# Output projection of a decoder trunk: x loaded behind the next operands, four sums of squares together, turns a step later, U2 added to the rows by GpSimd

## The chip, the cores and the metric

The kernel runs on one core of one Trainium2 chip. The metric is the device time of one execution in microseconds; the lower the better. A core has TensorE (matmuls and transposes, into eight banks of PSUM), VectorE, ScalarE, GpSimd and SyncE (SP), which here only issues DMAs. Each engine runs its own instructions in order and waits on semaphores of the others.

## The reference

One layer of a hybrid decoder trunk on 1024 tokens of width 1024, in float32. What matters here is the end of the token-mixing sub-layer and the norm behind it:

```python
def rmsnorm(x, g):
    xf = x.astype(jnp.float32)
    y = xf * lax.rsqrt(jnp.mean(xf * xf, axis=-1, keepdims=True) + RMS_EPS)
    return (y * g.astype(jnp.float32)).astype(x.dtype)
...
    x = x + merged @ w_o
    h2 = rmsnorm(x, norm2_g)
    g_ff, up_ff = jnp.split(h2 @ w_gate_up, 2, axis=-1)
    return x + (jax.nn.silu(g_ff) * up_ff) @ w_down
```

`merged` (the four mixers' branches, weighed by gates) is 1024 x 1024, and so is `w_o`.

## The kernel before, in words

Each float32 matmul is made of three: both operands are split into a high part (a cast on ScalarE, L143) and a low part (the difference, on VectorE, L144), and hi·hi, lo·hi and hi·lo are added up in PSUM (L138 to L140). `split` and `split2` do this for operands in `hi`/`lo` tiles or in halves of `ohl`.

The output projection `outproj` multiplies 2 x 2 blocks of 512 with seven block products instead of eight (Winograd's form). The list `OUT` has 28 steps: each is one product (na, nb) and one of four slices j of its inner dimension. A step has four tiles t of 128 rows and three matmuls for each, so 12 matmuls. I number the steps from 0. Steps 0 to 7 are the products 0 and 1, mixed, and then come the products 4 (steps 8 to 11), 3 (12 to 15), 6 (16 to 19), 5 (20 to 23) and 2 (24 to 27). A product has four banks of PSUM, `acc`, and after its last step each of the four is read out and added to what it belongs to.

The sums go into two sets of rows that were loaded from x: `x2[0]`, the first 512 tokens as four tiles of 128 x 1024, and `x2[1]`, the second 512. In the profile these tiles are called raw. A partial sum `u` is kept in the tile `part`: product 0, then U2 (product 4 added), later product 5. `x0` and `x1` are a row tile's two halves of columns.

`want_o(fetched, ready)` issues the operands' loads on SP (L997 the left half from `mfd` in DRAM, L998 the right half from `wo` or `wod`) up to eight steps ahead, and their splits up to six steps ahead. x is loaded by `load_x2`, four DMAs of 512 KB on SP (L850); the norm's weights `g2`, spread over 128 partitions, by one DMA on ScalarE's queue (L1042).

When a row tile of the first half is complete (after product 6), `norm2_first` normalizes and turns it: a square with its sum on ScalarE (L168), the power −1/2 on GpSimd (L164, behind a small VectorE instruction, L163), the scaling on VectorE (L1060, output xn), eight 128 x 128 transposes on TensorE (L1054, output trn), two copies out of PSUM (L1071) and their split into g0h and g0l. A copy f of the turned rows is kept. `beside(n)`, called in step 20 + n, advances these four generators: one tile a step is normalized, and is turned in the step after. In the steps 25 to 27 it prepares the first weights of the feed-forward layer. Behind `outproj` come twelve products on the first half's rows alone (`early`), beside which the second half is normalized and turned, and then the feed-forward layer's main loops.

What sets the order: loads stand on SP in the order of the code. Of the other engines' instructions a scheduler makes the final order when the program is built, by the order of the code, by dependencies and by a buffer pool: tiles of tag b share 14 buffers, and a tile waits for the last reader of the buffer that it takes. In `early` alone the matmuls and transposes are held in the order of the code.

Of the kernel before, what the change touches and what calls it, by code (L numbers as in the profile page):

```python
# [37 lines left out]
ALU = mybir.AluOpType  # L38
AX = mybir.AxisListType

P = 128
# [11 lines left out]
def tile_hybrid_trunk(  # L53
# [17 lines left out]
    nc = tc.nc  # L71
# [14 lines left out]
    def big(name, tag="b", dt=F32):  # L86
        return mn.tile([P, 1024], dt, tag=tag, name=name, bufs=NB[tag])
# [4 lines left out]
    def halves(v):  # L92
        return [v[:, :512], v[:, 512:]]
# [41 lines left out]
    def mm3(o, a, b, start, stop):  # L135
        ah, al = a
        bh, bl = b
        nc.tensor.matmul(o, ah, bh, start=start, stop=False)  # L138
        nc.tensor.matmul(o, ah, bl, start=False, stop=False)  # L139
        nc.tensor.matmul(o, al, bh, start=False, stop=stop)  # L140

    def split(hi, lo, v):
        nc.scalar.copy(hi, v)  # L143
        nc.vector.tensor_sub(lo, v, hi.bitcast(F32))  # L144
# [17 lines left out]
    def rstd_of(ss, n):  # L162
        nc.vector.tensor_scalar(ss, ss, 1.0 / n, EPS, op0=ALU.mult, op1=ALU.add)  # L163
        nc.gpsimd.tensor_tensor(ss, ss, nhalf[:, :ss.shape[1]], op=ALU.pow)  # L164

    def norm_stat(xt, xn):
        ss = sp.tile([P, 1], F32, name="ss")
        nc.scalar.activation(xn, xt, AF.Square, accum_out=ss)  # L168
        rstd_of(ss, D)
        return ss  # L170
# [9 lines left out]
    def h_tiles(name):  # L180
        hh = hp.tile([P, NK, HT], F32R, tag="hh", name=name + "h")
        hl = hp.tile([P, NK, HT], F32R, tag="hl", name=name + "l")
        return hh, hl
# [623 lines left out]
    add, sub, mul, tt = ALU.add, ALU.subtract, ALU.mult, nc.vector.tensor_tensor  # L807
    def bank(name):
        return pq.tile([P, HT], F32, tag="bank", name=name, bufs=8)
# [38 lines left out]
    def load_big(src):  # L848
        raw = big("raw")
        nc.sync.dma_start(raw, src)  # L850
        return raw

    def blocks_w(row0, row1, first=True):

        r0, r1 = load_big(row0), load_big(row1)
        s23, s14 = big("s23"), big("s14")
        s = halves(s14)[:1] + halves(s23) + halves(s14)[1:]
        four(s, *halves(r0), *halves(r1), True)
        w = {}
        if first:  # L860
            x = split2(r0)
            w[1], w[2] = half_of(x, 0), half_of(x, 1)
        x = split2(s23)
        w[6], w[7] = half_of(x, 0), half_of(x, 1)
        x = split2(s14, "b")
        w[5], w[3] = half_of(x, 0), half_of(x, 1)
        w[4] = halves(big("a22", "b", F32R))
        split(*w[4], halves(r1)[1])
        return w
# [123 lines left out]
    def want_o(fetched, ready):  # L993
        for na, nb, j in OUT[len(oraw):fetched]:
            r = big("or")
            if j < 3 or na > 1:
                nc.sync.dma_start(r[:, lo_], mfd[j][:, na])  # L997
            nc.sync.dma_start(r[:, hi_], wo[(0, 0, 1)[nb], j][:, (lo_, hi_, hi_)[nb]] if nb < 3 else wod[j][:, nb])  # L998
            oraw.append(r)
        for i in range(len(oops), min(ready, len(OUT))):  # L1000
            if i % 8 < 2:
                oops.append(split2(oraw[i]))
            else:
                v = t8([2, 1024], "ohl")
                oops.append([v[:, 0], v[:, 1]])
                split(*oops[i], oraw[i])

    load_x2 = lambda half: [load_big(x[half * HT + t * P:half * HT + (t + 1) * P, :]) for t in range(4)]
# [29 lines left out]
    stash = [dp.tile([P, D], F32, name=f"stash{g}") for g in range(EARLY)]  # L1038
    ffd = [dp.tile([P, 7, HT], F32, name=f"ffd{j}") for j in range(NF // 2)]
    wdd = [dp.tile([P, 7, HT], F32, name=f"wdd{j}") for j in range(NF // 2)]  # L1040
    g2 = big("g2")
    nc.scalar.dma_start(g2, norm2_g.partition_broadcast(P))  # L1042
    x2 = [load_x2(0), None]
    hA = h_tiles("g0")
    part = hp.tile([P, 8, HT], F32, tag="hl", name="part")
    hB = h_tiles("g1")
# [3 lines left out]
    def turn(xn, b):  # L1050
        tr = bank("trn")
        for k in range(4):
            kk = 4 * b + k
            nc.tensor.transpose(c4(tr)[:, k, :], xn[:, kk * P:(kk + 1) * P], identf)  # L1054
        return tr

    def norm2(x2):
        xn = big("xn2")
        ss = norm_stat(x2, xn)
        nc.vector.scalar_tensor_tensor(xn, x2, ss, g2, op0=ALU.mult, op1=ALU.mult)  # L1060
        return xn

    def norm2_first(t, x2):

        c = slice(t * P, (t + 1) * P)
        xn = norm2(x2)
        yield
        f1.append(big("f1"))
        for b in range(2):
            f = halves(f1[t])[b]  # L1070
            nc.scalar.copy(f, turn(xn, b))  # L1071
            split(hA[0][:, 4 * b:4 * b + 4, c], hA[1][:, 4 * b:4 * b + 4, c], c4(f))
            yield

    def norm2_second(t, x2):

        c = slice(t * P, (t + 1) * P)
        xn = norm2(x2)
        yield
        f11, f21 = halves(f1[t])  # L1080
        s = halves(big("s12")) + halves(big("s34"))
        tt(s[0], turn(xn, 0), f11, op=sub)
        split(hB[0][:, 0:4, c], hB[1][:, 0:4, c], c4(s[0]))
        yield
        tr = turn(xn, 1)
        tt(s[1], tr, s[0], op=sub)
        split(hB[0][:, 4:8, c], hB[1][:, 4:8, c], c4(tr))
        tt(s[2], s[1], f11, op=sub)
        tt(s[3], f21, s[1], op=sub)
        for v, to in zip(s[1:], (F.t2, F.t3, F.t4)):  # L1090
            split(to[0][:, :, c], to[1][:, :, c], c4(v))
        yield

    def outproj(after):
        u, u4 = ([part[:, i + t] for t in range(4)] for i in (0, 4))
        accs = {}
        for i, (na, nb, j) in enumerate(OUT):
            want_o(i + 8, i + 6)
            if na not in accs:
                accs[na] = [bank("acc") for _ in range(4)]  # L1100
            X = accs[na]
            for t in range(4):
                tl = slice(t * P, (t + 1) * P)
                mm3(X[t], [v[:, tl] for v in oops[i]], [v[:, hi_] for v in oops[i]], j == 0, j == 3)
            for t in range(4) if j == 3 else ():
                x0, x1 = (v and halves(v[t]) for v in x2)
                if na == 0:
                    nc.scalar.copy(u[t], X[t])
                    nc.gpsimd.tensor_tensor(x0[0], x0[0], u[t], op=add)
                elif na == 1:  # L1110
                    tt(x0[0], X[t], x0[0], op=add)
                elif na == 4:
                    tt(u[t], X[t], u[t], op=add)
                elif na == 3:
                    tt(u4[t], X[t], u[t], op=add)
                    tt(x1[1], X[t], x1[1], op=add)
                    nc.gpsimd.tensor_tensor(x0[1], x0[1], u4[t], op=add)
                elif na == 6:
                    tt(x0[1], X[t], x0[1], op=add)
                    nc.gpsimd.dma_start(x2d[t], x2[0][t])  # L1120
                elif na == 5:
                    tt(u[t], X[t], u[t], op=add)
                else:
                    tt(x1[0], X[t], x1[0], op=add)
                    for c in x1:
                        tt(c, c, u[t], op=add)
                    nc.gpsimd.dma_start(x2d[4 + t], x2[1][t])
            if i == 8:
                x2[1] = load_x2(1)
            if i >= 20:  # L1130
                after(i - 20)

    def prepared(f):
        return split2(load_big(wgu[f]))
# [10 lines left out]
        nc.gpsimd.dma_start(stash[g], st)  # L1145

    up_w = lambda g: blocks_w(wgu[2 * g], wgu[2 * g + 1], g >= EARLY)
    turns = [norm2_first(t, x2[0][t]) for t in range(4)]
    ready = []

    def beside(n):

        if n < 4:
            next(turns[n])
        if 0 < n < 5:
            next(turns[n - 1])
            next(turns[n - 1])
        if n >= 5:
            ready.append(prepared(2 * (n - 5)))

# [4 lines left out]
    turns = [norm2_second(t, x2[1][t]) for t in range(4)]  # L1165
# [77 lines left out]
    v, u = (hp.tile([P, 8, HT], F32, tag="hl", name=n) for n in ("pu", "ug"))  # L1243
# [68 lines left out]
    def pool_add(o, v):  # L1312
        nc.gpsimd.tensor_tensor(o, o, v, op=add)
# [8 lines left out]
    with in_order([(nc.tensor, "matmul"), (nc.scalar, "copy"), (nc.scalar, "activation"), (nc.sync, "dma_start")]):  # L1322
        X = product(0, each(load_xr))
        for t in range(4):
            nc.scalar.copy(p1[t], X[t])
        X = product(1, each(load_xr, range(4, 8)) + each(lambda t: pool_add(xr[t][:, lo_], p1[t])))
        for t in range(4):
            tt(xr[t][:, lo_], X[t], xr[t][:, lo_], op=add)
        X = product(2, each(lambda t: first_half(t, lo_)))
        for t in range(4):  # L1330
            tt(u2[t], X[t], p1[t], op=add)
        X = product(3)
# [4 lines left out]
        X = product(4)  # L1337
# [4 lines left out]
        X = product(5, each(lambda t: first_half(4 + t, hi_)))  # L1342
        for t in range(4):
            tt(xr[4 + t][:, lo_], X[t], xr[4 + t][:, lo_], op=add)
        X = product(6, each(last_half), stagger=6)
    with in_order():
# [5 lines left out]
        x, ss = xr[3], ssf[3]  # L1352
# [74 lines left out]
```

## Time and profile before

| what | value |
|---|---|
| median of 3 runs | 1564.3 us (1563.82 to 1564.4) |
| the profiled execution: time, span of its instructions | 1562.95 us, 1561.2 us |
| granted TensorE clock | 0.998 |
| busy share of the span: TensorE, VectorE, ScalarE, GpSimd | 99%, 78%, 43%, 13% |
| output projection, first matmul to the first behind it | 834.2 to 921.0 us |

The times in the trace are microseconds from the start of the span. A row of the timeline has the start, the length, the engine, the line of the kernel, the operation, output and inputs by their names, and in brackets how long the engine was idle before it, and what ended that. A matmul's length is longer than the distance to the next one's start, since matmuls are pipelined; what it takes of the engine is that distance. A count at the end (x4) tells how many equal instructions were merged into one row.

### The profile page before, as it was taken

The page shows a single profiled execution, that of the slowest core. Times are in us where ns is not written, and L with a number is a line of the kernel's source. Part 1 is how long each engine was busy: PE and PEld are TensorE (multiplying, and loading weights), DVE is VectorE, ACT ScalarE, POOL GpSimd, SP SyncE. Part 2 cuts the span into 40 slices and gives each one's busy share as a digit, 9 for nine tenths or more (in the row PEclk, how much of TensorE's full clock was granted, in tenths as well). Part 3 has the DMA queues.
Part 4 walks back from the last instruction along what each step waited for, and adds up shares of the span by engine and source line. Part 5 has one row for each costly group of instructions (what it writes and reads, how often), then busy time and mean ns, then how long its engine had stood idle before and what let it go on. Part 6 is the DMA issues. An engine that isn't in the chain of part 4 may idle for free.

```text
span 1561.2 us, 20401 instructions
## 1 busy us (share of the span) xinstructions
PE 1540.8 (99%) x7362; PEld 1274.3 (82%) x7362; DVE 1212.7 (78%) x1811; ACT 663.6 (43%) x1083; POOL 203.3 (13%) x327
## 2 busy tenths in 40 slices
PE   9999999999999999999999989999999999999998
PEld 8878878888788888888887878888888888888887
DVE  7585687786966878888986878888898888666566
ACT  6343355664666633333333456321222222354343
POOL 2011021221122100000001221000011111110410
PEclk9999999999999999999999999999999999999999
DMA  5221311101346744545447755355465555998612
GB/s 190 71 78 35 103 34 37 34 23 34 128 153 221 270 133 150 184 148 182 155 162 260 269 206 189 141 196 183 162 222 209 209 211 214 342 409 310 191 55 108
DMA packets 94456, 258.05 MB, mean 165 GB/s; under 512 B 11185, under 2 KB 16465, under 8 KB 94354
## 3 DMA queue, kind: packets, MB, share of 16 engines
q1 hardware_dynamic: 73104, 182.80, 34.8%
q0 software_dynamic: 20816, 72.63, 11.7%
q8 instruction: 58, 0.95, 0.2%
q10 hardware_dynamic: 434, 1.32, 0.2%
q14 instruction: 44, 0.36, 0.1%
HBM read 177.25 MB, written 79.45 MB: 164 GB/s over the span
## 4 chain that ended last, share of the span: by engine, by line
PE 86%; DVE 5%; issue 4%; DMA 2%; ACT 2%; POOL 0%; SPq 0%; DVEq 0%; ACTq 0%; POOLq 0%
PE acc L154 13%; PE pp L138 13%; PE pp L140 13%; PE pp L139 13%; PE mm L138 5%; PE mm L140 4%; PE mm L139 4%; PE pp L154 4%; PE o L512 2%; PE trp L499 2%; PE mmz L154 1%; PE pc L139 1%; PE pc L140 1%; PE z L441 1%; PE acc L139 1%
## 5 line engine op out<-in xcount | busy, mean ns | idle before, releaser
L143 ACT CAST hi<-s 128x1024 fp32r<-128x1024 f32 x76 | 76.7, 1050 | 182.1 <-DVE s L823 166.5
L154 PE MATMUL acc<-dhl 128*128 128x512 f32 (+1 forms) x558 | 125.8, 382 | 0.0
L154 PEld LDWEIGHTS acc<-dhl 128*128 128x128 f32 x558 | 102.5, 188 | 20.4
L144 DVE TENSOR_TENSOR lo<-s,hi 128x1024 fp32r<-128x1024 f32 x76 | 90.1, 1221 | 13.5 <-ACT hi L143 13.4
L144 DVE TENSOR_TENSOR dhl<-dr,dhl 128x1024 fp32r<-128x1024 f32 x45 | 58.5, 1312 | 34.0 <-ACT dhl L154 34.0
L890 ACT ACTIVATE g<-g 128x512 f32<-128x512 f32 x38 | 23.9, 629 | 125.9 <-DVE g L889 113.4
L144 DVE TENSOR_TENSOR lo<-raw,hi 128x1024 fp32r<-128x1024 f32 x46 | 55.9, 1219 | 22.5 <-ACT hi L143 22.5
L138 PE MATMUL mm<-h0h,whi 128*128 128x512 f32 x176 | 72.7, 413 | 0.0
L138 PE MATMUL mm<-h1h,whi 128*128 128x512 f32 x176 | 72.4, 412 | 0.1
L154 ACT CAST dhl<-dr 128x1024 fp32r<-128x1024 f32 x45 | 47.2, 1055 | 58.5 <-PE acc L154 22.7
L139 PE MATMUL mm<-h1l,whi 128*128 128x512 f32 x176 | 70.5, 401 | 0.0
L140 PE MATMUL mm<-h0h,wlo 128*128 128x512 f32 x176 | 70.0, 398 | 0.0
L139 PE MATMUL mm<-h0l,whi 128*128 128x512 f32 x176 | 69.8, 396 | 0.0
L140 PE MATMUL mm<-h1h,wlo 128*128 128x512 f32 x176 | 69.2, 393 | 0.0
L138 PE MATMUL pp<-g1h,hi 128*128 128x512 f32 x176 | 68.5, 389 | 0.0
L139 PE MATMUL pp<-g1l,hi 128*128 128x512 f32 x176 | 68.5, 389 | 0.0
L140 PE MATMUL pp<-g1h,lo 128*128 128x512 f32 x176 | 68.5, 389 | 0.0
L143 ACT CAST hi<-raw 128x1024 fp32r<-128x1024 f32 x46 | 48.1, 1051 | 44.6 <-DMA raw<-in_wgu_dram 31.7
L144 DVE TENSOR_TENSOR pt<-trp,pt 128x512 fp32r<-128x512 f32 (+1 forms) x80 | 50.5, 633 | 14.8 <-ACT pt L143 13.7
L143 ACT CAST pt<-trp 128x512 fp32r<-128x512 f32 (+1 forms) x80 | 43.7, 546 | 41.3 <-PE trp L499 25.6
L138 PE MATMUL pp<-t2h,hi 128*128 128x512 f32 x152 | 59.1, 389 | 0.0
L139 PE MATMUL pp<-t2l,hi 128*128 128x512 f32 x152 | 59.1, 389 | 0.0
(440 smaller groups left out, 4579.9 us busy)
## 6 DMA issues: line engine op xcount, KB each, us to landing
raw<-in_wgu_dram SPq DMA_DIRECT2D x56, 512.0 KB, 4.5
dr<-ffd SPq DMA_DIRECT2D x77, 256.0 KB, 5.1
raw<-in_wgate_dram SPq DMA_DIRECT2D x32, 512.0 KB, 5.3
raw<-prd SPq DMA_DIRECT2D x32, 512.0 KB, 3.4
wraw<-in_wmix_dram SPq DMA_DIRECT2D x22, 512.0 KB, 3.6
ffd<-fs POOLq DMA_DIRECT2D x22, 512.0 KB, 4.4
raw<-in_wd_dram SPq DMA_DIRECT2D x22, 512.0 KB, 3.7
wdd<-fs POOLq DMA_DIRECT2D x22, 512.0 KB, 3.5
```

Of the source, the lines that this page charges most:

```text
L138: nc.tensor.matmul(o, ah, bh, start=start, stop=False)
L139: nc.tensor.matmul(o, ah, bl, start=False, stop=False)
L140: nc.tensor.matmul(o, al, bh, start=False, stop=stop)
L143: nc.scalar.copy(hi, v)
L144: nc.vector.tensor_sub(lo, v, hi.bitcast(F32))
L154: setattr(e, n, lambda *a, _f=f, **k: tc.keep_in_program_order(_f(*a, **k)))
L441: nc.tensor.matmul(z[:, :f], qs[:, j, ql], kk[j][:, u0:u0 + f], start=True, stop=False)
L499: nc.tensor.transpose(tr[:, (1 - s) * 256 + e * P:(1 - s) * 256 + (e + 1) * P], pq[e][:, (s0 + s) * P:(s0 + s + 1) * P], identf)
L512: nc.tensor.matmul(o, vv[:, s0 + s, j, :], pt[:, i, (1 - s) * 256:(2 - s) * 256], start=s0 + s - i == ns - 1, stop=s0 + s - i == -1)
L890: nc.scalar.activation(g0[:, 512:], g0[:, 512:], act)
```

## The change

The first half's rows of x are loaded behind the operands of steps 8 and 9 (in step 2 of the code) rather than ahead of them, and the second half's behind those of steps 16 and 17 (in step 10 rather than 8). `g2` is loaded on SP behind the latter. GpSimd adds U2 to the first half's right columns after product 4, and VectorE adds product 3 to the same columns directly; before, VectorE made U2 plus product 3 in a tile of its own (`u4`), and GpSimd added that. `norm2_first` pauses between its sum of squares and its scaling; `beside` starts all four sums of squares and the first two scalings in step 20, the other scalings in 21 and 22, and turns the tiles in the steps 22 to 25 (before: 21 to 24).

```diff
-    g2 = big("g2")
-    nc.scalar.dma_start(g2, norm2_g.partition_broadcast(P))
-    x2 = [load_x2(0), None]
+    x2, g2 = [None, None], []
@@ norm2_first
-        xn = norm2(x2)
+        xn = big("xn2")
+        ss = norm_stat(x2, xn)
+        yield
+        nc.vector.scalar_tensor_tensor(xn, x2, ss, g2[0], op0=ALU.mult, op1=ALU.mult)
         yield
@@ outproj
-        u, u4 = ([part[:, i + t] for t in range(4)] for i in (0, 4))
+        u = [part[:, t] for t in range(4)]
...
                 elif na == 4:
                     tt(u[t], X[t], u[t], op=add)
+                    nc.gpsimd.tensor_tensor(x0[1], x0[1], u[t], op=add)
                 elif na == 3:
-                    tt(u4[t], X[t], u[t], op=add)
+                    tt(x0[1], X[t], x0[1], op=add)
                     tt(x1[1], X[t], x1[1], op=add)
-                    nc.gpsimd.tensor_tensor(x0[1], x0[1], u4[t], op=add)
...
-            if i == 8:
+            if i == 2:
+                x2[0] = load_x2(0)
+            if i == 10:
                 x2[1] = load_x2(1)
+                g2.append(big("g2"))
+                nc.sync.dma_start(g2[0], norm2_g.partition_broadcast(P))
@@ beside
-        if n < 4:
-            next(turns[n])
-        if 0 < n < 5:
-            next(turns[n - 1])
-            next(turns[n - 1])
+        if n == 0:
+            turns.extend(norm2_first(t, x2[0][t]) for t in range(4))
+            for t in (0, 1, 2, 3, 0, 1):
+                next(turns[t])
+        elif n < 3:
+            next(turns[n + 1])
+        if 1 < n < 6:
+            next(turns[n - 2])
+            next(turns[n - 2])
```

The lines of the changed kernel are one or a few higher, or lower: L1112 is L1111 of before (product 1's sums), L1120 is L1119 (product 6's), L1123 is L1122 (product 5's), L1125 is L1124 (product 2's), L1067 the scaling of the first half (L1060 before), L1052 the transposes (L1054), L1072 their copies (L1071).

ScalarE, from the last casts of step 7's operand to those of the steps 10 to 15, before:

```order
L143 CAST ohl<-or 128x512
L1042 DMA g_7537<-in_norm_g_dram 128x1024
L1108 COPY part<-acc 128x512 x4
L143 CAST hi<-or 128x1024 x2
L143 CAST ohl<-or 128x1024 x6
```

and in the changed kernel:

```order
L143 CAST hi<-or 128x1024
L1109 COPY part<-acc 128x512
L143 CAST hi<-or 128x1024
L1109 COPY part<-acc 128x512 x3
L143 CAST ohl<-or 128x1024 x6
```

The high part of step 8's operand moves ahead of the four copies of product 0, and that of step 9 ahead of the last three. On VectorE at the same place, from the sums for the last quarter of `merged`, before:

```order
L823 TENSOR_TENSOR fs<-fs,raw 128x512
L825 TENSOR_TENSOR fs<-raw,fs 128x512
L1111 TENSOR_TENSOR raw<-acc,raw 128x512 x4
L144 TENSOR_TENSOR lo<-or,hi 128x1024 x2
L144 TENSOR_TENSOR ohl<-or,ohl 128x1024 x4
```

and in the changed kernel:

```order
L823 TENSOR_TENSOR fs<-fs,raw 128x512
L825 TENSOR_TENSOR fs<-raw,fs 128x512
L144 TENSOR_TENSOR lo<-or,hi 128x1024 x2
L1112 TENSOR_TENSOR raw<-acc,raw 128x512 x4
L144 TENSOR_TENSOR ohl<-or,ohl 128x1024 x3
```

Both low parts move ahead of product 1's four sums. On VectorE around the scalings of the first half (the numbers behind xn tell the four tiles apart: 7992, 8013, 8051, 8090 before, 7992, 7997, 8002, 8007 after), before:

```order
L163 TENSOR_SCALAR ss<-ss 128x1
L144 TENSOR_TENSOR ohl<-or,ohl 128x1024
L163 TENSOR_SCALAR ss<-ss 128x1
L144 TENSOR_TENSOR ohl<-or,ohl 128x1024
L1060 SCALAR_TENSOR_TENSOR xn_7992<-raw,ss,g_7537 128x1024
L1060 SCALAR_TENSOR_TENSOR xn_8013<-raw,ss,g_7537 128x1024
L1122 TENSOR_TENSOR part<-acc,part 128x512 x2
L144 TENSOR_TENSOR g0l<-f_8019,g0h 128x4x128 x2
L1122 TENSOR_TENSOR part<-acc,part 128x512
L163 TENSOR_SCALAR ss<-ss 128x1
L1122 TENSOR_TENSOR part<-acc,part 128x512
L1060 SCALAR_TENSOR_TENSOR xn_8051<-raw,ss,g_7537 128x1024
```

and in the changed kernel:

```order
L163 TENSOR_SCALAR ss<-ss 128x1
L1067 SCALAR_TENSOR_TENSOR xn_7992<-raw,ss,g_7770 128x1024
L1067 SCALAR_TENSOR_TENSOR xn_7997<-raw,ss,g_7770 128x1024
L163 TENSOR_SCALAR ss<-ss 128x1
L144 TENSOR_TENSOR ohl<-or,ohl 128x1024
L163 TENSOR_SCALAR ss<-ss 128x1
L1067 SCALAR_TENSOR_TENSOR xn_8002<-raw,ss,g_7770 128x1024
L144 TENSOR_TENSOR ohl<-or,ohl 128x1024
L1067 SCALAR_TENSOR_TENSOR xn_8007<-raw,ss,g_7770 128x1024
L144 TENSOR_TENSOR g0l<-f_8046,g0h 128x4x128 x2
L1123 TENSOR_TENSOR part<-acc,part 128x512 x4
L144 TENSOR_TENSOR g0l<-f_8079,g0h 128x4x128 x2
```

All four scalings now stand ahead of the first split of a turned tile (g0l) and of product 5's sums (L1123). Ahead of these rows, product 6's sums (L1120) now alternate with the low parts of steps 22 to 24, where L1119 stood behind those of steps 21 to 24. On TensorE the transposes of the four tiles stood ahead of the last tile of step 23, one matmul later, ahead of step 24 and ahead of step 25; in the changed kernel they stand ahead of step 23, ahead of step 24, in step 25 (behind its second matmul) and ahead of step 26.

More of the change, by code (lines that the diff above doesn't have):

```diff
@@ L1059, in norm2 @@
         ss = norm_stat(x2, xn)
-        nc.vector.scalar_tensor_tensor(xn, x2, ss, g2, op0=ALU.mult, op1=ALU.mult)
+        nc.vector.scalar_tensor_tensor(xn, x2, ss, g2[0], op0=ALU.mult, op1=ALU.mult)
         return xn
@@ L1065, in norm2_first @@
         c = slice(t * P, (t + 1) * P)
-        xn = norm2(x2)
+        xn = big("xn2")
+        ss = norm_stat(x2, xn)
+        yield
+        nc.vector.scalar_tensor_tensor(xn, x2, ss, g2[0], op0=ALU.mult, op1=ALU.mult)
         yield
@@ L1147, in tile_hybrid_trunk @@
     up_w = lambda g: blocks_w(wgu[2 * g], wgu[2 * g + 1], g >= EARLY)
-    turns = [norm2_first(t, x2[0][t]) for t in range(4)]
-    ready = []
+    turns, ready = [], []
     def beside(n):
-        if n < 4:
-            next(turns[n])
-        if 0 < n < 5:
-            next(turns[n - 1])
-            next(turns[n - 1])
+        if n == 0:
[7 more added lines that the diff above has]
+            next(turns[n - 2])
         if n >= 5:
```

## The prediction

> **What bounds the kernel now.** First the busy time by stretch (columns: stretch in us, its length, then busy us and instruction count of TensorE matmuls, weight loads, VectorE, ScalarE, GpSimd, the granted clock, DMA share, GB/s), then who TensorE waited for (total, times, longest), then the timeline of the engines.
>
> ```profile
> 856.00:922.00 66.00, 59.94 (x279) 49.03 (x278) 56.31 (x69) 35.20 (x47) 15.14 (x15) 1.00 0.65 230
> 1000.00:1200.00 200.00, 200.00 (x884) 165.67 (x883) 169.30 (x230) 48.08 (x61) 17.09 (x32) 1.00 0.52 187
> 1200.00:1400.00 200.00, 200.00 (x884) 165.68 (x883) 158.51 (x196) 70.91 (x85) 25.71 (x38) 1.00 0.71 267
> 1400.00:1520.00 120.00, 120.00 (x532) 99.38 (x531) 76.02 (x83) 51.12 (x61) 20.96 (x12) 1.00 0.58 198
> ...
> PE trn L1054 <- DVE xn L1060: 4.1, 2, 3.6
> PE acc L139 <- DVE lo L144: 2.0, 1, 2.0
> ```
>
> TensorE is the bound: behind the output projection it is busy in every microsecond to 1520, at full clock. So time won in the output projection goes through to the end, and nothing else of the change counts. There TensorE idles 6.06 of 66 us, in two places:
>
> ```profile
> 834.17 0.39 PE L138 MATMUL acc<-hi 128*128 128x512 f32 x1
> ...
> 856.15 1.07 PE L138 MATMUL acc<-hi 128*128 128x512 f32 x4
> 859.22 0.50 PE L139 MATMUL acc<-lo,hi 128*128 128x512 f32 x1 [2.00 <-DVE lo L144]
> ...
> 901.10 0.39 PE L140 MATMUL acc<-ohl 128*128 128x512 f32 x1
> 901.93 1.09 PE L1054 MATMUL trn<-identf,xn 128*128 128x128 f32 x8 [0.44 <-DVE xn L1060]
> 902.77 0.48 PE L138 MATMUL acc<-ohl 128*128 128x512 f32 x1
> ...
> 904.28 0.40 PE L140 MATMUL acc<-ohl 128*128 128x512 f32 x1
> 908.29 1.06 PE L1054 MATMUL trn<-identf,xn 128*128 128x128 f32 x8 [3.61 <-DVE xn L1060]
> ...
> 921.01 0.39 PE L154 MATMUL pp<-g0h,hi 128*128 128x512 f32 x1
> ```
>
> 884 matmuls in 200 us are 0.226 us from start to start, so a step of 12 takes 2.72; eight transposes take 0.84 (901.93 to 902.77). By starts, the first wait costs 859.22 − 856.15 − 4 × 0.227 = 2.16, the second 901.93 − 901.10 − 0.227 = 0.60, the third 908.29 − 904.28 − 0.227 = 3.78: 6.54 together. No version can win more here.
>
> **Part 1: x loaded behind the next operands; the first wait.** What step 8 waits for is the low part of its operand (L144) on VectorE:
>
> ```profile
> 851.59 2.63 ACT L1108 COPY part<-acc 128x512 f32<-128x512 f32 x4 [9.70 <-PE acc L140]
> 854.11 2.00 ACT L143 CAST hi<-or 128x1024 fp32r<-128x1024 f32 x2
> ...
> 852.26 5.05 POOL L1109 TENSOR_TENSOR raw<-raw,part 128x512 f32<-128x512 f32 x4 [2.36 <-DMA or<-wod]
> ...
> 854.36 1.37 DVE L1111 TENSOR_TENSOR raw<-acc,raw 128x512 f32<-128x512 f32 x2 [5.29 <-PE acc L140]
> 857.34 0.69 DVE L1111 TENSOR_TENSOR raw<-acc,raw 128x512 f32<-128x512 f32 x1 [0.56 <-POOL raw L1109]
> 857.95 2.35 DVE L144 TENSOR_TENSOR lo<-or,hi 128x1024 fp32r<-128x1024 f32 x2
> 860.22 4.62 DVE L144 TENSOR_TENSOR ohl<-or,ohl 128x1024 fp32r<-128x1024 f32 x4
> ...
> 837.36 3.73 SPq L850 DMA_DIRECT2D raw<-in_x_dram  x4
> 841.89 0.33 SPq L997 DMA_DIRECT2D or<-mfd  x1
> 847.67 0.32 SPq L998 DMA_DIRECT2D or<-wod  x1
> 854.33 0.32 SPq L997 DMA_DIRECT2D or<-mfd  x1
> 859.40 2.71 SPq L850 DMA_DIRECT2D raw<-in_x_dram  x4
> ...
> or<-wod SPq DMA_DIRECT2D x16, 256.0 KB, 4.0
> raw<-in_x_dram SPq DMA_DIRECT2D x8, 512.0 KB, 7.3
> g<-in_norm_g_dram ACTq DMA_DIRECT2D x1, 512.0 KB, 7.9
> ```
>
> (The last three rows are DMA issues: count, KB each, median us to landing.) The low part waits behind the four L1111 on VectorE, and these for GpSimd's four adds (1.26 each). In the changed order both low parts stand ahead of the evacuations, and the cast of step 8 ahead of the first L1108 on ScalarE. Their loads start where x's did, so they are issued by 837 to 839 and land by 843, or by 847 if 7.9 instead of 4.0. VectorE is idle before 854.36 for 5.29 us, so step 8's low part ends by about 850; it is needed at 856.4. Step 9's cast (1.0) comes behind the first copy and ends by 853.2, its low part by 854.4; needed 858.9. The wait goes: **−2.16**.
>
> What is late next: x lands after issue at 839 to 843 plus 7.3, by 850; the first add starts at 852.26 as before. One cast between the copies puts the second copy at 853.7, the adds end at 857.5 and the four evacuations at 858.3 (858.0 before). Behind them on VectorE are the low parts of steps 10, 11, 12 (1.155 each: 859.5, 860.6, 862.2), needed at 861.6, 864.4, 867.1. The load at 854.33 (step 11) is held by a store of fs to memory, before and after; its cast came at 857.8. No wait. GpSimd's and VectorE's instructions are as many as before.
>
> g2's load leaves ScalarE's queue and stands on SP behind x's second half. There x comes two operands later: I take 863.5 to 866.5 for its four issues (859.40 before, plus two operand pairs of about 1 us each and a wait for an operand to land), so x lands by 874; g2, issued by 867, lands by 875. x is read from step 15's end on, 876.3; g2 at 894. What stands behind on SP are operands 18 to 21, the last held until g2 has landed, so issued at 875 and landed by 879; needed at 891.5. Cost 0 by that cover; bounds 0 and what rival D gives.
>
> **Part 2: U2 added by GpSimd a product earlier; four squares at once; turns later.** These go together, since the scheduler re-sorts VectorE's and ScalarE's rows by them.
>
> ```profile
> 887.72 2.54 POOL L1117 TENSOR_TENSOR raw<-raw,part 128x512 f32<-128x512 f32 x2 [2.36 <-DVE part L1115]
> 879.18 2.21 POOL L1117 TENSOR_TENSOR raw<-raw,part 128x512 f32<-128x512 f32 x1 [21.87 <-DVE part L1115]
> ...
> 889.36 4.26 DVE L144 TENSOR_TENSOR ohl<-or,ohl 128x1024 fp32r<-128x1024 f32 x3
> 894.68 2.47 DVE L1119 TENSOR_TENSOR raw<-acc,raw 128x512 f32<-128x512 f32 x4
> 900.60 2.47 DVE L1060 SCALAR_TENSOR_TENSOR xn<-raw,ss,g 128x1024 f32<-128x1024 f32 x2
> 906.86 1.28 DVE L1060 SCALAR_TENSOR_TENSOR xn<-raw,ss,g 128x1024 f32<-128x1024 f32 x1
> ...
> 904.62 1.07 ACT L168 ACTIVATE xn<-raw 128x1024 f32<-128x1024 f32 x1
> 906.28 0.55 POOL L164 TENSOR_TENSOR ss<-ss,nhalf 128x1 f32<-128x1 f32 x1 [5.18 <-DVE ss L163]
> ```
>
> Before, the last sums of the rows (L1119) stand behind four low parts and start at 894.68; two more low parts stand ahead of the first scaling, at 900.60. The third square (904.62) stands on ScalarE behind the copies of the transposes, so its scaling at 906.86 is what TensorE waited for at 908.29. Now the squares come between the casts, ahead of those copies.
>
> I follow the new order with these durations, on TensorE's new clock: step k starts at 856.15 + 2.72 (k − 8), and a tile's sum is read 1.1 us after the step's first matmul (step 6 starts at 834.17 + 6 × 2.72 = 850.5, first copy 851.59). Step 11: 864.3, first L1114 at 865.4; with five low parts of 1.155 and four L1114 of 0.60, VectorE is through step 17's low part at 873.6. GpSimd's adds trail it: the fourth starts at 872.7 and ends by 875 at 2.21, or 874 at 1.27. Step 15: 875.2, first L1117 at 876.3, eight sums at 0.60 to 881.1; then the low parts of steps 18 to 21, 882.2 for the first, needed at 883.6: **1.4 us to spare**. Low parts end at 885.7, the sums of step 19 (starts 886.1) run 887.2 to 893.0 with steps 22 to 24 between. Squares on ScalarE begin when their buffers come free (a low part each): 890.7, 892.8, 894.7; the fourth needs the first scaling's buffer, 895.6 to 896.7. GpSimd issues four stores (0.55 each) and the first power, done at 894.2; the first scaling is 894.3 to 895.5, the others at 896.7, 899.3, 901.8.
>
> TensorE's transposes now stand ahead of step 23 (856.15 + 15 × 2.72 = 897.0), ahead of 24 (900.6), in 25 (904.7) and ahead of 26 (908.0). So each has its rows 1.5, 3.9, 5.4 and 6.2 us early. Two more waits are new. The third tile's transposes need the bank that L1123 frees, behind the first tile's low halves: 901.8 + 1.2 + 0.6 = 903.7 against 904.7, 1.0 to spare. And at the end the first early product's weights' low part (L144 lo<-raw) now stands behind the first L1125, which reads the last step: step 27 starts at 911.7, its first sum is read at 912.9 to 913.5, the low part ends at 914.7 against 914.9 for the third matmul: 0.2 us below or above zero, bounds 0 and one low part, 1.2. I take 0.2. Hence **−(0.60 + 3.78) + 0.2 = −4.2**. Behind it the second weight operand is due 5.4 us later, the others later still, and the first transposes of the second half 16 us later.
>
> Sum: −2.16 − 4.18 = **−6.3 us**. The profiled execution has a span of 1561.2 and a time of 1562.95, which would become 1556.6; it ran 1.35 us below the median of the runs, so against 1564.3 I say **1558.0**.
>
> **The rivals.** A is the forecast; its own range is 1557.2 to 1559 (all 6.54 and 0.6 of spread at one end; one low part at the end and one slip of a margin at the other).
>
> B: GpSimd's adds collide with VectorE's splits, now beside steps 12 to 17. For it: the lone add took 2.21 beside splits and 1.27 otherwise, and there
>
> ```profile
> 868.13 1.22 DVE L144 TENSOR_TENSOR ohl<-or,ohl 128x1024 fp32r<-128x1024 f32 x1
> ...
> 880.75 1.72 DVE L144 TENSOR_TENSOR ohl<-or,ohl 128x1024 fp32r<-128x1024 f32 x1
> ```
>
> a split took 1.72, not 1.22. Four times 0.5 is 2.0 on VectorE, inside its 2.7 (873.6 to 876.3), so nothing. If each of five splits waits out an add of 1.27, VectorE is 6.4 later, which passes 2.7 + 1.4 by 2.3: 1558.0 + 2.3 = 1560.3. [...]
>
> C: no measurable change. The second stall stays, since the first scaling or the bank comes late: a slip of over 1.5 us between 887 and 895 is enough to start it, and 5.9 us (1.5 + 4.4) would eat the whole second gain. Then only −2.2 is left: 1562.1. Against it: before, that lateness came from the queue positions of L1119 and of the third square, both gone.
>
> D: slower. x's second half, behind two more operands, lands late; L1118 needs it, ahead of step 18's low part. From 877.7 on (876.3 + 1.4) each microsecond later is one of TensorE; past 884 the gain is gone, past 887.2 the kernel is measurably slower, so a landing 21 us after issue against the 7.3 of the row. With 23 it would be 1566. For it only that the DMA queue is crowded there; the row is a median.
>
> **How the numbers follow.** A 0.74, B 0.09, C 0.11, D 0.06. A measurement tells 0.2%, 3.1 us, from no change: A and B are faster (0.83), C the same (0.11), D slower (0.06). The time is A's. The range holds A and B and reaches a part of the way to C: 1557.0 to 1561.0.
>
> **What would show it.** After: no TensorE wait for a low part near step 8 and none for xn; the last step's end 6.3 us earlier; GpSimd's U2 adds near 866 to 875; squares close together ahead of the copies of the transposes; at most a short wait at the first early product. I am wrong if TensorE waits at step 18 for a low part, at the third tile's transposes for L1123, or if an operand of steps 18 to 21 lands past its step.

## The result, and the profile after

The changed kernel takes 1555.9 us (median of 4 runs, 1554.47 to 1556.13) against 1564.35 for the kernel before beside it; the ratio is 0.9942, 95% interval 0.9931 to 0.9954. Five more runs in a later set gave 1556.22 against 1564.61, 0.9947 (0.9933 to 0.9960). So the gain is 8.4 us, where 6.3 was forecast, and the time lies 1.1 below the range. Its profiled execution took 1554.47, with a span of 1552.8.

The busy time by stretch, of the kernel after (columns as in the prediction; the column behind GpSimd is the granted clock):

```profile
856.00:916.00 60.00, 60.00 (x283) 49.99 (x282) 53.26 (x67) 34.00 (x46) 15.59 (x14) 1.00 0.67 244
1000.00:1200.00 200.00, 200.00 (x884) 165.64 (x883) 172.57 (x234) 50.43 (x64) 18.16 (x34) 1.00 0.52 191
1200.00:1400.00 200.00, 200.00 (x884) 165.59 (x884) 157.77 (x197) 73.54 (x92) 24.65 (x36) 1.00 0.74 276
1400.00:1510.00 110.00, 110.00 (x487) 91.10 (x486) 68.69 (x73) 44.76 (x49) 20.96 (x12) 1.00 0.55 186
```

TensorE no longer idles in the output projection: 60.00 of 60 us, where it was busy 59.94 of 66. The list of its waits (total, times, longest) has lost both rows of the projection; of the longest ones left, the second row is the start of the program, and the other two are, but for 0.4, waits near 420, some 400 us ahead of the projection:

```profile
PE pc L139 <- DVE ylo L144: 1.8, 2, 1.4
PE warm L154 <- POOL identf masks.py:199: 1.5, 1, 1.5
PE pc L138 <- DVE xa L739: 0.6, 1, 0.6
```

The timeline of TensorE after: the projection's first matmul, the transposes, and the first matmul behind it:

```profile
832.58 0.39 PE L138 MATMUL acc<-hi 128*128 128x512 f32 x1
...
895.33 1.03 PE L1052 MATMUL trn<-identf,xn 128*128 128x128 f32 x8
...
898.94 1.03 PE L1052 MATMUL trn<-identf,xn 128*128 128x128 f32 x8
...
903.01 0.60 PE L1052 MATMUL trn<-identf,xn 128*128 128x128 f32 x4
...
906.21 1.03 PE L1052 MATMUL trn<-identf,xn 128*128 128x128 f32 x8
...
912.53 0.39 PE L154 MATMUL pp<-g0h,hi 128*128 128x512 f32 x1
```

No row has a bracket. The projection takes 912.53 − 832.58 = 79.95 us; before it took 921.01 − 834.17 = 86.84. That is 6.89 of the 8.4. The profiled execution of after also reaches the projection 1.59 earlier than that of before, through code in which nothing was changed, and behind the projection both need the same: 1552.8 − 912.53 = 640.27 and 1561.2 − 921.01 = 640.19 (640.2 in every profile of this case). So a run's span is a start, a projection and 640.2 us. I compare the kernels by the middle term.

VectorE after, with the rows that the prediction's steps speak of:

```profile
847.41 1.22 DVE L144 TENSOR_TENSOR lo<-or,hi 128x1024 fp32r<-128x1024 f32 x1
851.53 1.48 DVE L144 TENSOR_TENSOR lo<-or,hi 128x1024 fp32r<-128x1024 f32 x1 [2.90 <-ACT hi L143]
...
865.90 1.72 DVE L144 TENSOR_TENSOR ohl<-or,ohl 128x1024 fp32r<-128x1024 f32 x1
...
869.78 2.31 DVE L144 TENSOR_TENSOR lo<-or,hi 128x1024 fp32r<-128x1024 f32 x1
...
872.62 1.21 DVE L144 TENSOR_TENSOR lo<-or,hi 128x1024 fp32r<-128x1024 f32 x1
874.51 0.69 DVE L1117 TENSOR_TENSOR raw<-acc,raw 128x512 f32<-128x512 f32 x1 [0.69 <-PE acc L140]
...
879.31 4.62 DVE L144 TENSOR_TENSOR ohl<-or,ohl 128x1024 fp32r<-128x1024 f32 x4
...
892.87 2.48 DVE L1067 SCALAR_TENSOR_TENSOR xn<-raw,ss,g 128x1024 f32<-128x1024 f32 x2 [0.40 <-POOL ss L164]
...
899.33 1.28 DVE L1067 SCALAR_TENSOR_TENSOR xn<-raw,ss,g 128x1024 f32<-128x1024 f32 x1
...
911.48 1.22 DVE L144 TENSOR_TENSOR lo<-raw,hi 128x1024 fp32r<-128x1024 f32 x1
```

### The profile page after: what moved, and what is told of

Read it like the earlier page. It is cut to its first block, busy times and chain, and to the rows that moved or that the text cites. A ratio compares the mean times of both kernels' runs of the same rounds, so it can differ in the third digit from the quotient of the medians.

```text
span 1552.8 us, 20394 instructions
## 1 busy us (share of the span) xinstructions
PE 1538.5 (99%) x7362; PEld 1273.3 (82%) x7362; DVE 1213.0 (78%) x1811; ACT 662.9 (43%) x1083; POOL 206.2 (13%) x327
## 4 chain that ended last, share of the span: by engine, by line
PE 93%; DVE 3%; ACT 1%; issue 1%; DMA 1%; POOL 0%; SPq 0%; ACTq 0%; DVEq 0%; POOLq 0%
PE pp L140 14%; PE pp L139 14%; PE pp L138 14%; PE acc L154 14%; PE mm L138 5%; PE mm L140 5%; PE mm L139 5%; PE pp L154 4%; PE o L512 2%; PE trp L499 2%; PE acc L139 2%; PE acc L140 2%; PE acc L138 2%; PE mmz L154 1%; PE z L441 1%
## 5 line engine op out<-in xcount | busy, mean ns | idle before, releaser
L140 PE MATMUL pp<-t3h,lo 128*128 128x512 f32 x152 | 59.2, 389 | 0.0
L140 PE MATMUL pp<-t4h,a 128*128 128x512 f32 x152 | 59.2, 389 | 0.0
```

## The experiments

The profile of before has one place ahead of its end where the granted clock is not 1.00: 3.41 us at 0.50, behind a stretch of 3.42 in which TensorE was busy for 1.62.

```profile
418.33:421.75 3.42, 1.62 (x9) 0.99 (x8) 3.42 (x5) 2.15 (x4) 0.57 (x1) 1.00 0.89 323
421.75:425.16 3.41, 3.21 (x8) 2.53 (x9) 3.41 (x6) 2.41 (x4) 0.00 (x0) 0.50 0.07 30
```

Two theories stood against each other. T1: this is what idle TensorE brings on, so where it idles for some 2 us or more within 3.4 us, the next window of 3.4 us runs at half clock, and a wait costs more than its idle time, in some runs and not in others (such a window is called a spell in the expectations). T2: the 2 us beyond the forecast are luck of the runs. A run's mean granted clock tells roughly how many such windows it had: one takes 3.41 × 0.5 / 1561 = 0.0011 off. The clock is at half at the end too, where TensorE has nothing left to do: for the last 2.84 us in the profile of before and 5.23 in that of after, which takes 0.0009 and 0.0017 off. So by these numbers a mean clock of 0.999 means no such window, and 0.998 means none or one.

**The loads alone** (x behind the next operands, g2 on SP; no other part):

```diff
-    x2 = [load_x2(0), None]
+    x2, g2 = [None, None], []
...
-            if i == 8:
+            if i == 2:
+                x2[0] = load_x2(0)
+            if i == 10:
                 x2[1] = load_x2(1)
+                g2.append(big("g2"))
+                nc.sync.dma_start(g2[0], norm2_g.partition_broadcast(P))
```

> Before, with the loads alone moved (x behind the next operands, g2 on SP behind x's second half); squares, turns and U2 as before. Both theories: the first wait (2.16 us, step 8's low part) goes, the wait of 3.78 for the third tile's scaled rows stays. So -2.2 us, 1562.1, by both theories: T1 (each TensorE idle of about 3.8 us is followed in most executions by 3.4 us at half the granted clock, which costs 1.4 to 1.7 us more than the idle time) leaves that spell where it was. If the time falls by 5 or more, the loads also take away the second stall, and both are wrong on the parts.

Measured: 1559.67 against 1564.43, ratio 0.9966 (0.9954 to 0.9979): −4.8, more than both theories said, and close to the 5 that I had set for a second stall taken away whole, which lies in the interval. In its trace the first wait is gone, and the second wait, 3.61 before, is smaller:

```profile
901.08 1.09 PE L1052 MATMUL trn<-identf,xn 128*128 128x128 f32 x8 [0.53 <-DVE xn L1058]
...
904.98 1.06 PE L1052 MATMUL trn<-identf,xn 128*128 128x128 f32 x8 [2.11 <-ACT xn L168]
```

The projection takes 83.56, 3.28 less than before: 2.2 from the first wait and the rest from the second. Both theories were wrong in leaving the second wait whole; why it shrank, no run shows. The other 1.5 of the gain is no wait.

**Squares at once and turns later alone:**

```diff
+        xn = big("xn2")
+        ss = norm_stat(x2, xn)
+        yield
...
+        if n == 0:
+            turns.extend(norm2_first(t, x2[0][t]) for t in range(4))
+            for t in (0, 1, 2, 3, 0, 1):
+                next(turns[t])
...
```

> Before, with the four squares at once and the turns a step later alone; loads and U2 as before. The first wait (2.16) stays; the waits for scaled rows (0.60 and 3.78) go or shrink below 0.6. T1 (the clock answers to that idle): -4.4 from the idle and -1.4 from the spell that no longer follows it, -5.8, 1558.5. T2 (the extra 2 us of the change are luck of the runs, no spell hangs on this stall): -4.4 at most, 1559.9.

Measured: 1560.69 against 1564.43, 0.9974 (0.9964 to 0.9985): −3.7 (2.3 to 5.6), nearer to the number of T2 (−4.4 at most) than to that of T1 (−5.8). Its projection takes 83.52 (−3.32): the first wait stays at 2.01, a wait of 1.0 for the first scaling stays, the long one is gone.

**U2 by GpSimd alone:**

```diff
...
                     tt(u[t], X[t], u[t], op=add)
+                    nc.gpsimd.tensor_tensor(x0[1], x0[1], u[t], op=add)
...
-                    tt(u4[t], X[t], u[t], op=add)
+                    tt(x0[1], X[t], x0[1], op=add)
-                    nc.gpsimd.tensor_tensor(x0[1], x0[1], u4[t], op=add)
```

> Before, with U2 added to the rows by GpSimd after product 4 alone. VectorE's rows of step 20 stand behind the same four low parts as before, and the sums that moved end earlier than anything needs them. Both theories: no change, 1564.3 within 1 us. If it gains over 2 us, the last sums were held by GpSimd's add and not by the low parts ahead of them.

Measured: 1564.96, 1.0004 (0.9995 to 1.0013). No change of the time, as expected. Its profile does differ: the short wait ahead of the first transposes (0.44 in the row of before) is gone, and one window at half clock follows the longer wait; the projection takes 87.72. Of its 11 runs 9 had a mean clock of 0.996 or less, of the 23 of before 12, so a small gain may be hidden behind such windows.

**Work for TensorE in the longer wait**, with no wait taken away:

```diff
-    def turn(xn, b):
+    def turn(xn, b, idle=0):
         tr = bank("trn")
+        for _ in range(idle):
+            nc.tensor.transpose(c4(tr)[:, 0, :], identf, identf)
...
-            nc.scalar.copy(f, turn(xn, b))
+            nc.scalar.copy(f, turn(xn, b, 28 if t == 2 and b == 0 else 0))
```

> Before, with 28 more transposes of the identity (written to the bank that the next transposes overwrite, read by nobody; about 2.9 us of TensorE) right before the third tile's first transposes, so that TensorE works in most of the 3.78 us in which it waits for that tile's rows; all waits stay, and nothing of the output changes. T1 (the spell at half clock is started by the idle time itself): no spell behind it, -1.4 us, 1562.9, between -0.8 and -1.7 in the median. T2 (no spell hangs on it): no change or a few tenths slower, 1564.3 to 1564.8.

Measured: 1563.61 against 1564.43, 0.9995 (0.9986 to 1.0004): −0.8 with an interval that holds both theories. But 10 of its 11 runs had a mean clock of 0.998 or more, against 9 of 23 of the kernel before in the same set.

**The changed kernel again**, beside the next three:

> The changed kernel once more, beside the others of this set. Both theories: 1555.9, between 1554.4 and 1556.3. T1 (short TensorE idle starts spells of 3.4 us at half clock) expects two groups 1.4 to 1.7 us apart, without and with one spell, since one idle place of 2.0 us is left, near 420; and no run far above 1556.5, since the idle of the output projection is gone. T2 (luck of the runs) expects one broad group, and with more runs a median nearer to 1557 to 1558, as the sum said.

Measured: 1556.22 (1555.37 to 1557.12), projection 80.00. The median stayed where it was; the two separate groups that T1 named are not to be seen in five runs.

**Work in both waits:** the 28 transposes in the longer wait as above, and 18 in the first:

```diff
+                for _ in range(18 if i == 8 and t == 0 else 0):
+                    nc.tensor.transpose(X[t][:, :P], identf, identf)
                 mm3(X[t], [v[:, tl] for v in oops[i]], [v[:, hi_] for v in oops[i]], j == 0, j == 3)
```

> Before, with the 28 transposes in the wait of 3.78 us as in the earlier run, and 18 more (1.9 us) ahead of step 8's first matmuls, into a bank that these overwrite, so that TensorE works through the wait of 2.16 us as well. No wait is taken away; the projection keeps its 86.8 us. T1: neither place starts a spell, one is left near 420 as in the changed kernel; so the distance to the changed kernel is that of the projections alone, 6.9, and the time 1562.8, at a mean clock of 0.998 or more in nearly every run. T2: 1564.4, as before.

Measured: 1562.23 against 1564.61, 0.9986 (0.9978 to 0.9995): **2.4 us faster than before by adding work**. All 11 runs had a mean clock of 0.998 or 0.999 (9 of them 0.999), of the 15 runs of before beside them 6 (none 0.999). Its timeline shows the transposes where TensorE had idled, and the waits behind them ending where they did:

```profile
855.76 2.13 PE L1107 MATMUL acc<-identf 128*128 128x128 f32 x18
857.65 1.17 PE L138 MATMUL acc<-hi 128*128 128x512 f32 x4
858.83 0.50 PE L139 MATMUL acc<-lo,hi 128*128 128x512 f32 x1
...
904.08 3.22 PE L1053 MATMUL trn<-identf 128*128 128x128 f32 x28
907.76 1.09 PE L1056 MATMUL trn<-identf,xn 128*128 128x128 f32 x8 [0.46 <-DVE xn L1062]
```

The projection takes 86.73, as before (86.84). So the 2.4 come from no wait; they are the price that idle TensorE pays in the clock. Between this kernel and the changed one lie the waits alone: 6.0 by the medians of the same set, and 86.73 − 80.00 = 6.7 by the projections. T2 falls.

**The change without its part on U2:**

```diff
...
-                    nc.gpsimd.tensor_tensor(x0[1], x0[1], u[t], op=add)
...
-                    tt(x0[1], X[t], x0[1], op=add)
+                    tt(u4[t], X[t], u[t], op=add)
...
+                    nc.gpsimd.tensor_tensor(x0[1], x0[1], u4[t], op=add)
```

> The changed kernel without its part on U2 (VectorE makes U2 plus product 3, GpSimd adds it after product 3, as before). TensorE's order is that of the changed kernel. GpSimd's four adds start at about 877 and end by 882 to 886, ahead of the sums of the rows at 885 to 891. Both theories: no difference to the changed kernel, 1555.9 within 0.7. If it is 1 us or more slower, the fourth sum waits for GpSimd and U2's part is needed.

Measured: 1556.36, beside 1556.22 for the whole change; projection 79.96. Loads and turns make the whole gain; moving U2 is worth nothing that these runs can tell.

**A version that might be better still:** one low part near 420 on GpSimd.

```diff
-            split(*y[k], raw)
+            if i == 2 and k == 0:
+                nc.scalar.copy(y[k][0], raw)
+                nc.gpsimd.tensor_sub(y[k][1], raw, y[k][0].bitcast(F32))
+            else:
+                split(*y[k], raw)
```

> The changed kernel, with the first low part that the projection of the third branch (pc, near 420) waits for made by GpSimd, which is idle there, and not behind a scan on VectorE. GpSimd can start at 417.4 and takes about 2.5, so TensorE's wait of 1.37 ends 1.3 to 1.7 earlier; the small matmuls now ahead of it come behind it. T1: the idle time there falls from 2.0 to about 1 us in a window of 3.4 and starts no spell: -0.7 to -1.3 from idle time and -1 in the median from the spell, 1553.9, at a mean clock of 0.998 to 0.999, without a second group. T2: only the idle time, 1554.9. If GpSimd's write collides with VectorE's scans or the scans' own chain sets the pace, no gain: 1555.9.

Measured: 1555.83 (1554.98 to 1556.76) beside 1556.22: inside the spread of either. The wait that ended at 421.60 now ends at 420.50, but a second one follows, for the next low part, which still stands behind VectorE's other work:

```profile
420.50 0.50 PE L139 MATMUL pc<-ylo,wbr 128*128 128x512 f32 x1 [0.88 <-POOL ylo L773]
...
423.36 0.50 PE L139 MATMUL pc<-ylo,wbr 128*128 128x512 f32 x1 [0.64 <-DVE ylo L144]
```

Whether it beats the changed kernel stays undecided.

**Work in the first wait alone** (the 18 transposes without the 28):

> Before, with only the 18 transposes in the first wait (2.16 us, step 8); the wait of 3.78 us stays idle. T1: a wait of 2.16 us leaves a window of 3.4 us less than 40% busy in about a third of the phases, so half a spell's price is saved on average: 1563.7 to 1564.2, and runs at 0.995 become rare while runs at 0.996 and 0.997 stay. T3 (each of the two waits nearly always starts its spell): as much as filling the other wait, 1563.0 to 1563.6. T2 (no spell hangs on it): 1564.4.

Measured: 1564.00 against 1563.95, 1.0000 (0.9991 to 1.0009): no gain. By the time alone T1's 0.2 to 0.7, T2's nothing and the near end of T3's 0.8 to 1.4 all lie in the interval; T3 falls by the profiles, in which a window at half clock follows the first wait in only one of six executions (the table below). T1's guess that runs at a mean clock of 0.995 become rare was a miss: 2 of 11, against 1 of 15 of before beside them. That the same 18 transposes were worth 1.6 more when the other wait was filled too (2.4 against 0.8) lies within the two intervals, so the times don't settle the share of each wait. Its profiled execution shows the longer wait followed by two windows at half clock instead of one (its projection took 89.52):

```profile
903.40:906.81 3.41, 0.83 (x6) 0.40 (x4) 3.35 (x7) 3.41 (x8) 0.55 (x1) 1.00 0.48 150
906.81:910.22 3.41, 2.37 (x10) 2.30 (x11) 2.97 (x6) 2.79 (x7) 0.93 (x1) 0.50 0.44 135
910.22:913.63 3.41, 3.41 (x9) 2.64 (x9) 3.41 (x6) 1.09 (x2) 0.00 (x0) 0.50 0.50 177
```

**The kernel before, profiled twice more for its clock:**

> The kernel before, for its clock records alone. T1: spells of 3.41 us at half clock stand only behind the places with more than 1.9 us of idle within 3.4 us: near 421, 859 and 908. Of these the last most often. T2: spells anywhere, the earlier stages with their many short waits too.

> The kernel before, for its clock records, as in the look ahead of this: spells near 421, 859 and 908 or none by T1; anywhere by T2.

The first took 1563.58, with one window at half clock, behind the longer wait (908.02 to 911.43), and a projection of 88.44. The second took 1565.48, with three, behind the waits near 420, 857 and 907 and nowhere else. Its busy time in steps of 3.41 us around the projection's two waits (the number behind the length is TensorE's busy time, and in brackets its matmuls):

```profile
855.48:858.89 3.41, 1.40 (x7) 0.86 (x6) 2.81 (x4) 1.87 (x3) 1.25 (x2) 1.00 0.83 260
858.89:862.30 3.41, 3.41 (x9) 2.63 (x9) 3.41 (x4) 1.61 (x3) 0.00 (x0) 0.50 1.03 353
862.30:865.71 3.41, 3.41 (x16) 2.81 (x16) 1.97 (x2) 1.75 (x3) 0.00 (x0) 1.00 1.04 398
906.68:910.09 3.41, 0.83 (x9) 0.86 (x9) 3.34 (x6) 3.28 (x8) 0.55 (x1) 1.00 0.33 124
910.09:913.50 3.41, 3.41 (x11) 2.73 (x9) 2.97 (x6) 2.14 (x4) 0.93 (x1) 0.50 0.87 282
913.50:916.91 3.41, 3.41 (x20) 2.90 (x20) 2.34 (x5) 1.75 (x4) 0.00 (x0) 1.00 0.06 25
```

A window with TensorE busy for 1.40 or 0.83 of 3.41 is followed by one granted 0.50, in which 9 and 11 instructions fit where the next window takes 16 and 20. The timeline of that execution shows it behind the first wait, where a matmul starts every 0.43 us and then every 0.23:

```profile
858.65 0.61 PE L139 MATMUL acc<-lo,hi 128*128 128x512 f32 x1 [2.01 <-DVE lo L144]
859.05 0.63 PE L140 MATMUL acc<-hi,lo 128*128 128x512 f32 x1
859.48 0.63 PE L139 MATMUL acc<-lo,hi 128*128 128x512 f32 x1
...
862.40 0.39 PE L139 MATMUL acc<-lo,hi 128*128 128x512 f32 x1
862.62 0.39 PE L140 MATMUL acc<-hi,lo 128*128 128x512 f32 x1
...
923.57 0.39 PE L154 MATMUL pp<-g0h,hi 128*128 128x512 f32 x1
```

Its projection took 923.57 − 833.63 = 89.94, 3.10 more than the 86.84 of the execution that the prediction was made from: 1.55 for each window. Of the five profiled executions that have the longer wait whole, that one alone has no such window in the projection, though it has the same two waits. Its windows (carried on in steps of 3.413 us from the one at half clock at 421.75, see the next section for the step) happened to cut both:

```profile
855.24:858.65 3.41, 1.98 (x9) 1.31 (x7) 2.49 (x4) 2.65 (x3) 2.07 (x2) 1.00 0.88 276
...
903.03:906.44 3.41, 1.65 (x11) 1.13 (x10) 3.41 (x8) 3.41 (x8) 0.16 (x1) 1.00 0.26 71
906.44:909.85 3.41, 1.55 (x11) 1.50 (x12) 3.35 (x6) 3.25 (x7) 0.74 (x2) 1.00 0.33 117
909.85:913.26 3.41, 3.41 (x20) 2.85 (x19) 2.97 (x5) 2.14 (x5) 0.57 (x1) 1.00 0.81 273
```

The projections side by side, in us, with the windows at half clock in them:

| execution | projection | windows at half clock behind the first wait | behind the longer wait |
|---|---|---|---|
| before, the one of the prediction | 86.84 | 0 | 0 |
| before, second | 88.44 | 0 | 1 |
| before, third | 89.94 | 1 | 1 |
| U2 alone | 87.72 | 0 | 1 |
| work in the longer wait | 86.78 | 0 | 0, filled |
| work in the first wait | 89.52 | 0, filled | 2 |
| work in both waits | 86.73 | 0, filled | 0, filled |
| loads alone | 83.56 | wait gone | 0, wait of 2.11 left |
| turns alone | 83.52 | 0 | wait gone |
| changed kernel, twice | 79.95; 80.00 | wait gone | wait gone |
| changed kernel without U2; with a low part on GpSimd | 79.96; 79.95 | wait gone | wait gone |

So the first wait, left as it is, was followed by such a window in one of six executions, and the longer wait in four of five: together about one in each execution. One costs 1.5 to 1.6 us (U2 alone: 87.72 against 86.84 less the 0.60 of its missing short wait). By this count the loads alone should gain 3.3 of waits and some 1.5 of windows, and measured 4.8; the turns alone 3.3 and 1.2, and measured 3.7, short of the sum but with 4.5 inside their interval.

With 640.2 behind the projection, 833.9 ahead of it (mean of the twelve profiled executions that have the same code up to there, 832.6 to 834.9) and 1.7 between span and time, before's median of 1564.4 has a projection of 88.6: about one window at half clock in the middle run, which agrees with the count, though no profile of a middle run was taken. The median of after, 1556.0, has 80.2: none. The 53 executions of before beside the experiments agree too: they took 1562.0 on average at a mean clock of 0.999 (4 of them), 1563.9 at 0.998 (18), 1564.0 at 0.997 (9), 1565.2 at 0.996 (16) and 1565.9 at 0.995 (6).

## Why the prediction was right or wrong

**The first wait: right.** Its low part ended at 848.63 (850.2 on before's clock, since after's trace runs 1.59 ahead; "ends by about 850" was said), the second one started at 851.53; no wait.

**The margins: right to within 0.3 us, but for the one that rival B speaks of.** On before's clock the first low part of step 18 starts at 880.9 and ends at 882.1 (said: 882.2), the first scaling ends at about 895.7 (895.5), the transposes start at 896.9, 900.5, 904.6 and 907.8 (897.0, 900.6, 904.7, 908.0). x's second half was issued at 859.48 to 861.67 and landed within 7.4 us, long before 876: rival D had no ground. (Its price was off by its own terms, too: if a landing 21 us after issue gives 1564.3 + 3.1, one after 23 gives about 1569.5, not 1566.) At the end the low part was at hand, and the 0.2 that I added for it wasn't paid.

**Rival B: the collision is there and does no harm.** GpSimd's four adds took 2.20 to 2.28 each beside the splits, and three splits took 1.72, 1.71 and 2.31 where 1.22 is usual: 2.1 us in all, which used most of VectorE's spare time. Its next sum still waited 0.69 for TensorE (874.51). The rows beside those above:

```profile
864.17 1.22 DVE L144 TENSOR_TENSOR ohl<-or,ohl 128x1024 fp32r<-128x1024 f32 x1
868.15 1.71 DVE L144 TENSOR_TENSOR ohl<-or,ohl 128x1024 fp32r<-128x1024 f32 x1
...
864.33 6.67 POOL L1115 TENSOR_TENSOR raw<-raw,part 128x512 f32<-128x512 f32 x3 [7.66 <-DVE part L1114]
872.77 2.20 POOL L1115 TENSOR_TENSOR raw<-raw,part 128x512 f32<-128x512 f32 x1 [1.76 <-DVE part L1114]
```

In these rows the one that comes second ends about 1.1 us after the other has ended, as if it had stood still until then. The first three adds end at 866.54, 868.78 and 871.00, and the splits that began beside them (865.90, 868.15, 869.78) end 1.08, 1.08 and 1.09 later; a split alone takes 1.155 (879.31). The fourth add, begun at 872.77 beside the split of 872.62, ends 1.14 after that split. So the split of 1.72 in the prediction's row, half a us over the usual, need not speak against such a standstill: what each of the three splits waits out is what is left of the add when it comes (0.64, 0.63 and 1.22). Rival B's term, five splits that each wait out an add of 1.27, is shown by no run: these three waited, 2.1 us in all. The sum by the rows stood.

**Part 2, U2's share.** I took U2, squares and turns together. The runs show U2 to be worth nothing by itself (1564.96) or in the whole (1556.36 without it).

**The step that failed is the last one of the sum**: "it ran 1.35 us below the median of the runs, so against 1564.3 I say 1558.0", and with it "No version can win more here". I took what the profiled execution ran below the median as something that stays. It was a part of the stalls: that execution had no window at half clock in its projection, the middle run of before has about one (88.6 against 86.84), and the change removes the waits that start it. So the term that the sum put at nothing is this window, 1.5 to 1.6 us about once a run; filling both waits without removing them measured it at 2.4 us (0.8 to 3.4 by the interval). A smaller part of the miss is the size of the waits: 6.3 in the sum, 6.9 in the projections of before and after, which are the 0.2 not paid and some 0.35 that no single row accounts for. A part of that are matmuls further apart right behind a wait (0.33 to the next, not 0.23, at 858.83 with work in both waits).

After's profiled execution, too, ran 1.4 below its median, 1554.47 against 1555.9, as if the offset had stayed after all. But it has another source: that execution reached the projection at 832.58, 1.3 ahead of the mean of 833.9, and its projection (79.95) is that of the other executions of after. What the two profiled executions ran below their medians is alike by chance.

The windows are read from the clock itself: where an execution has half clock more than once, its starts lie whole multiples of one step apart. The two windows at 0.50 of the third profile of before start at 858.89 and 910.09, 51.20 us or 15 × 3.413 apart, and the one near 420 at 421.98, 436.91 or 128 × 3.413 ahead of the first; with work in the first wait alone it is 422.12 and 906.81, 484.69 or 142 × 3.413. The windows in which the clock stayed full are these steps carried on. And a gap of 2.01 us in the wait's row (858.65) was enough where it fell into one window, the one with 1.40 busy.

## What to carry to other kernels

In this kernel a wait of TensorE of 2 us or more costs its length and, depending on where a 3.4 us window cuts it, up to 1.6 us more in the window behind it (once 2.7, in two windows: 89.52 against 86.84); so one profile may show less than its average price. Before a sum is carried from the profiled execution to the median, the mean clock of all runs should be held against that of the profiled one: what lies between them may hang on the very wait that is removed. More than one profile of the kernel before would have shown it here. Where a wait can't be removed, transposes of an identity into a bank that is overwritten anyway buy the clock back (2.4 us here), and they tell the two prices apart.

## What was not expected of the hardware

In these profiles the half clock goes with the share of a window that TensorE is busy, not with one long gap: near 420 no single wait is longer than 1.4 (1.36 in the first profile of before), and yet half clock follows there, while the projection's window of that profile with 1.55 busy, idle for the other 1.86 in one piece, was not followed by it. In the projection, over all the profiles, the two windows at full clock with 1.38 (U2 alone) and 1.40 us busy (third profile of before), and those with 0.70 and 0.83, were followed by half clock, and those with 1.45 (loads alone), 1.55, 1.65, 1.76 and all above were not. Near 420 the border lay elsewhere: six windows with 1.54 to 1.86 were followed by it, and those with 1.87 and 2.03 to 2.06 were not. So the values part at each place, but at another number, and the profile's busy time alone doesn't tell what follows; what else counts stays open. In the one execution where a window at half clock was itself 2.37 busy (work in the first wait), the next was granted half again, where behind 3.21 and 3.41 the clock was full again: there 2.37 was not enough to return, while 1.45 at full clock had been enough to stay. And a window of 0.50 near 420 cost less than 1.55: the six executions with one reach the projection at 834.3 on average (833.6 to 834.9), the six without at 833.6 (832.6 to 834.5). That TensorE waits for others there anyway would explain it, but no run shows it.
